# A hybrid decoder layer on one core: 4 KB of descriptor scratch instead of 16, and one to four more buffers for five kinds of tiles

## The chip, the core and the metric

The kernel runs on one core of a Trainium2 chip. The core has a matrix engine (TensorE, PE in the profile, with PEld for the loading of its weights), VectorE (DVE), ScalarE (ACT), GpSimd (POOL) and SyncE (SP), which each work through their own instructions in order and wait for each other by semaphores. DMAs are issued from the queues of SP, ACT and POOL and run on 16 DMA engines. The metric is the device time of one execution in microseconds; less is better.

## The reference, cut to what matters

One inference step of a decoder layer for a prompt (1024 tokens) and for 8 samples with 4 new tokens each. Each sample has a past of 8192 keys in pages of 128 that lie scattered in a pool. The attention has three branches: compressed blocks, the 16 best blocks of 64 keys, and a sliding window.

```python
def compress(k, pe, w1, w2):
    ...
    per = jnp.einsum('bcjgd,rjdh->rbcgh', kc, w1r)
    ...
    return jax.nn.silu(h) @ w2
...
    _, idx = lax.top_k(score, n_top)
    ...
    k_sel = ks_bg[b_i, g_i, idx].reshape(B, N_KV, Q, n_sel, HEAD_DIM)
    v_sel = vs_bg[b_i, g_i, idx].reshape(B, N_KV, Q, n_sel, HEAD_DIM)
...
    q, kv, g_nsa, g_a, glu, g_b, g_mrg = split_cols(xn @ w_in, SPLITS)
```

So all the past keys and values of every sample are read page by page and compressed (the first cost), and the chosen blocks are gathered again from other pools (the second). Beside that stand one wide projection of 1056 tokens by `w_in`, a depthwise convolution, and the output products. Products in 32 bits are made of three: the operand is split into a rounded part ("h") and the rest ("l"), and hh, hl and lh are added.

## The kernel before

The program is written out as straight code, with a scheduler that sets the order of each engine's instructions from a timeline of its own and from priorities (`high_priority`). It knows how many buffers a tile has: a tile with the tag X and `bufs=N` may exist N times, and the instruction that fills the next one waits until the last reader of the oldest is done.

Stage one (up to about 530 us in the trace) weaves two streams (line 890). `units` compresses the samples' pages: the keys of samples 0 to 3, their values, the keys of samples 4 to 7, the choice of blocks, their values. `fill1` makes the first projections of `w_in`. In `compress` (line 509) one sample's keys or values are 16 gathers. A gather (line 573) is an indirect DMA of POOL that fills a tile `G` of 128 rows by 512 numbers, of which there are GB. VectorE transposes it (line 531) into a quarter of `T` (two buffers); ScalarE rounds the four quarters into `Th` (line 535); VectorE subtracts them for `Tl` (line 539); TensorE then makes 24 products `x<-Th` or `x<-Tl` (line 521). 64 such groups of four gathers make up the eight samples. VectorE's order of these is pulled forward (HD at line 530).

A projection (`project`, line 250) loads 128 columns of `w_in` into `wt` on SP's queue (line 247), splits them into `wh` (ScalarE) and `wl` (VectorE), and makes 72 products `mm<-xh,wh`, `mm<-xl,wh`, `mm<-xh,wl` (lines 192 to 194).

Stage two (about 530 to 870 us) weaves the samples' selected and window attention, more projections, and the convolution's taps on VectorE (line 1264). Selected keys are gathered by POOL into `KG` (KB buffers, line 1043), ScalarE takes out one group's half into `kg` (K2 buffers, line 1046), and TensorE transposes it (line 1049). Values come into `VG`. The window's keys are loaded by SP into `wk` (WK buffers, line 962) and transposed on TensorE (line 968). From there on the prompt's attention, the merge and the output follow; none of the tiles whose buffers change is used after the last projections, in the first part of the prompt's attention.

## Time and profile before

| what | value |
| --- | --- |
| median of 3 runs | 1442.09 us (1439.83 to 1443.89) |
| the profiled execution | 1445.79 us, of which 1444.0 lie between its first and its last instruction |
| PE busy | 1349.5 us (93%), PEld 1206.3 (84%) |
| DVE busy | 1081.8 us (75%) |
| ACT busy | 721.4 us (50%) |
| POOL busy | 656.4 us (45%) |
| bytes moved by DMA | 256.86 MB, of which 125.85 by POOL's queue |

A row of a group gives line, engine, operation, what it writes and reads, its shape and count, then its busy time and the mean of one in ns, then the idle time of the engine ahead of it and what ended that. "x<-Tl,w1hk" writes x and reads Tl and w1hk. A row of waits gives who waited for whom, the total in us, how often, and the longest. A busy PE is not PE at its peak, since products overlap and their ends are modelled.

### The profile page before, as it was taken

To read this page: it belongs to the slowest core of one execution; us is meant where nothing else is said; L and a number is where in the kernel's file an instruction comes from. 1 tells how busy PE (TensorE), PEld (TensorE's weight loads), DVE (VectorE), ACT (ScalarE), POOL (GpSimd) and SP (SyncE) were. 2 spreads that over 40 slices of the span, in tenths; PEclk is the share of its full clock that TensorE was granted. 3 is DMA by queue.
4 is the path that set the end of the run, shared out by engine and by line. 5 is a ranking of instruction groups with operands and counts; after the bars stand their busy time and mean duration, and the time that the engine had idled before them with its cause. 6 is when DMAs were issued, how large, how long until landed. Compare 5 with 4: busy or idle time off the path is not lost.

```text
span 1444.0 us, 25602 instructions
## 1 busy us (share of the span) xinstructions
PE 1349.5 (93%) x9689; PEld 1206.3 (84%) x9689; DVE 1081.8 (75%) x1915; ACT 721.4 (50%) x1323; POOL 656.4 (45%) x537
## 2 busy tenths in 40 slices
PE   5999989979998999999999999999969999899997
PEld 4987889978898999878787889888958899789876
DVE  7787887787887765979864943978777987888233
ACT  5444455454442542445555424777656776653311
POOL 1477775777777434455544401444474221321200
PEclk9999999999999999999999999999989999999999
DMA  7565567556656536697878656533573632416421
GB/s 238 164 203 170 176 177 217 187 173 201 200 172 209 164 91 224 209 321 258 298 281 302 215 160 170 171 113 106 151 193 96 197 119 91 140 29 216 171 96 47
DMA packets 184357, 256.86 MB, mean 178 GB/s; under 512 B 27347, under 2 KB 137507, under 8 KB 183970
## 3 DMA queue, kind: packets, MB, share of 16 engines
q1 hardware_dynamic: 137114, 121.42, 28.1%
q0 software_dynamic: 36608, 125.85, 26.4%
q10 hardware_dynamic: 10512, 7.96, 1.8%
q8 instruction: 76, 1.25, 0.4%
q14 instruction: 47, 0.39, 0.1%
HBM read 215.56 MB, written 44.20 MB: 180 GB/s over the span
## 4 chain that ended last, share of the span: by engine, by line
PE 54%; DMA 15%; DVE 12%; issue 8%; POOL 6%; ACT 2%; SPq 2%; ACTq 0%; DVEq 0%; POOLq 0%
POOL G L573 6%; PE mm L192 5%; PE mm L194 5%; PE mm L193 5%; DMA G<-in_cache_k_cmp,idxc 5%; DMA G<-in_cache_v_cmp,idxc 4%; PE v L192 3%; PE v L194 3%; PE v L193 3%; PE tr L192 3%; PE tr L194 3%; PE tr L193 3%; DVE T L531 3%; PE tr L1512 2%; PE x L1032 2%
## 5 line engine op out<-in xcount | busy, mean ns | idle before, releaser
L192 PE MATMUL mm<-xh,wh 128*128 128x352 f32 x840 | 278.7, 332 | 3.6 <-DVE stg L284 2.0
L193 PE MATMUL mm<-xl,wh 128*128 128x352 f32 x840 | 275.3, 328 | 0.7 <-DVE xl L407 0.7
L194 PE MATMUL mm<-xh,wl 128*128 128x352 f32 x840 | 275.8, 328 | 0.0
L531 DVE STREAM_TRANSPOSE T<-G 128x512 f32<-128x512 f32 x260 | 175.2, 697 | 81.0 <-DMA G<-in_cache_k_cmp,idxc 38.6
L573 POOL DMA_INDIRECT G<-in_cache_k_cmp,idxc x128 | 164.7, 1287 | 99.5 <-DMA w2bk<-in_w_k 34.5
L573 POOL DMA_INDIRECT G<-in_cache_v_cmp,idxc x128 | 174.3, 1362 | 78.2 <-DVE T L531 45.4
L535 ACT ACTIVATE Th<-T 128x2048 fp32r<-128x2048 f32 x66 | 124.7, 1890 | 168.0 <-DVE T L531 123.1
L192 PEld LDWEIGHTS mm<-xh,wh 128*128 128x128 f32 x840 | 159.9, 190 | 13.1 <-issue 7.4
L194 PEld LDWEIGHTS mm<-xh,wl 128*128 128x128 f32 x840 | 159.9, 190 | 7.0 <-issue 6.7
L193 PEld LDWEIGHTS mm<-xl,wh 128*128 128x128 f32 x840 | 160.2, 191 | 6.5 <-issue 4.8
L1227 DVE SCALAR_TENSOR_TENSOR acc<-ub,dwT,acc 128x1024 f32<-128x1024 f32 x120 | 154.3, 1286 | 1.1
L539 DVE TENSOR_TENSOR Tl<-T,Th 128x2048 fp32r<-128x2048 f32 x66 | 146.9, 2225 | 3.0 <-ACT Th L535 2.9
L1335 DVE TENSOR_TENSOR ptl<-tr,pth 128x512 fp32r<-128x512 f32 (+1 forms) x152 | 100.3, 670 | 21.5 <-ACT pth L1334 20.5
L1426 ACT ACTIVATE P<-S,sc 128x640 f32<-128x640 f32 (+7 forms) x128 | 89.2, 701 | 36.8 <-PE tr L1512 19.1
L1334 ACT ACTIVATE pth<-tr 128x512 fp32r<-128x512 f32 (+1 forms) x152 | 87.6, 585 | 37.0 <-PE tr L1512 29.4
L1019 POOL DMA_INDIRECT KG<-in_cache_k_slc,idxs x56 | 66.0, 1179 | 81.9 <-ACT kg L1046 60.8
L1487 POOL TENSOR_SCALAR P<-P,sc 128x640 f32<-128x640 f32 (+4 forms) x32 | 53.0, 1656 | 109.7 <-DVE sc L1480 79.6
L521 PE MATMUL x<-Tl,w1hk 128*128 128x256 f32 (+1 forms) x264 | 78.2, 296 | 15.1 <-DVE Tl L539 11.1
L521 PE MATMUL x<-Tl,w1hv 128*128 128x256 f32 (+1 forms) x264 | 79.0, 299 | 10.7 <-DVE Tl L539 10.7
L1019 POOL DMA_INDIRECT VG<-in_cache_v_slc,idxs x56 | 64.3, 1148 | 51.3 <-PE y L1104 33.8
L1503 PE MATMUL acc<-ptl,vs 128*128 128x256 f32 x264 | 73.7, 301 | 10.9 <-DVE ptl L1335 10.5
L1512 PE MATMUL tr<-ident,P 128*128 128x128 f32 x528 | 81.5, 280 | 1.7 <-ACT var L1613 0.6
(469 smaller groups left out, 3593.2 us busy)
## 6 DMA issues: line engine op xcount, KB each, us to landing
wt<-in_w_in SPq DMA_DIRECT2D x42, 512.0 KB
m_d<-stg SPq DMA_DIRECT2D x16, 528.0 KB
x<-in_x_prompt SPq DMA_DIRECT2D x16, 512.0 KB
mb<-m_d SPq DMA_DIRECT2D x24, 176.0 KB
t_d<-mb SPq DMA_DIRECT2D x24, 176.0 KB
mb<-t_d SPq DMA_DIRECT2D x24, 176.0 KB
ma<-m_d SPq DMA_DIRECT2D x24, 176.0 KB
ldq<-qT_d SPq DMA_DIRECT2D x32, 128.0 KB
```

The costliest lines, as they stand in the source:

```text
L192: pe.matmul(ps, wh, xh, start=i == 0, stop=False)
L193: pe.matmul(ps, wh, xl, start=False, stop=False)
L194: LAST_MM[0] = pe.matmul(ps, wl, xh, start=False, stop=i == n - 1)
L521: pe.matmul(o, w[:, s], t[:, :, :, s // 2, s % 2], start=s == 0 and i == 0, stop=s == 7 and i == 2)
L531: dve.transpose(T[:, gi], G)
L535: act.activation(Th[:, :m], T[:, :m], AF.Copy)
L539: eng.tensor_tensor(Tl[:, r], T[:, r], Th.bitcast(F32)[:, r], op=ALU.subtract)
L573: pool.indirect_dma_start(out=G, out_offset=None, in_=tab, in_offset=bass.IndirectOffsetOnAxis(ap=idxc[:, b * 16 + gi:b * 16 + gi + 1], ax ...
L1019: pool.indirect_dma_start(out=dst, out_offset=None, in_=pools[n], in_offset=bass.IndirectOffsetOnAxis(ap=col, axis=0))
L1227: eng.scalar_tensor_tensor(a, x, dwT[:, ct, j:j + 1], a, op0=ALU.mult, op1=ALU.add)
L1335: dve.tensor_tensor(lo[:, :w], t[:, :w], hi.bitcast(F32)[:, :w], op=ALU.subtract)
L1512: pe.transpose(t[:, (2 * x + e) * 128:(2 * x + e + 1) * 128], Ps[e * 2 + i][:, c0:c0 + 128], ident)
```

## The change

```diff
-GB = 4
+GB = 8
...
-WK = 1
+WK = 2
...
-KB = 3
-K2 = 2
+KB = 4
+K2 = 3
...
-        wt = wpl.tile([128, 8, 128], F32, name="wt", tag="wt")
+        wt = wpl.tile([128, 8, 128], F32, name="wt", tag="wt", bufs=3)
...
-    nc = _bacc.Bacc("TRN2", target_bir_lowering=False, num_devices=1)
+    nc = _bacc.Bacc("TRN2", target_bir_lowering=False, num_devices=1, dynamic_dma_scratch_size=4096)
```

Since the scheduler counts buffers, it also orders the instructions anew. On POOL the last 64 gathers of stage one, the values of samples 4 to 7, are cut by two index tables for the choice of blocks (IOTA) and two fills of the convolution's input (MEMSET):

```order
 L573 DMA G<-in_cache_v_cmp,idxc 128x512 x64
 L573 DMA G<-in_cache_k_cmp,idxc 128x512 x64
-L573 DMA G<-in_cache_v_cmp,idxc 128x512 x3
+L573 DMA G<-in_cache_v_cmp,idxc 128x512 x8
 L173 IOTA TC 64x64
 L173 IOTA TA 128x128
-L573 DMA G<-in_cache_v_cmp,idxc 128x512 x19
+L573 DMA G<-in_cache_v_cmp,idxc 128x512 x20
 L1188 MEMSET ub 128x30 x2
-L573 DMA G<-in_cache_v_cmp,idxc 128x512 x42
+L573 DMA G<-in_cache_v_cmp,idxc 128x512 x36
```

The gathers follow each other as before; eight instead of three stand ahead of the tables, and 28 instead of 22 ahead of the fills.

On VectorE, in the compression of the first samples' keys (T is the transposition of one G, Tl the subtraction for a group of four, H the sums at a sample's end, wl a projection's weights), before:

```order
L531 STREAM_TRANSPOSE T<-G 128x512
L562 TENSOR_TENSOR H<-x,H 64x255
L562 TENSOR_TENSOR H<-x,H 64x256
L531 STREAM_TRANSPOSE T<-G 128x512 x3
L539 TENSOR_TENSOR Tl<-T,Th 128x2048
L531 STREAM_TRANSPOSE T<-G 128x512
L256 TENSOR_TENSOR wl<-wt,wh 128x1024
L566 SCALAR_TENSOR_TENSOR H<-sg,H 128x511
L531 STREAM_TRANSPOSE T<-G 128x512
L565 MEMSET H 128x1
L531 STREAM_TRANSPOSE T<-G 128x512 x2
L539 TENSOR_TENSOR Tl<-T,Th 128x2048
```

and of the change:

```order
L562 TENSOR_TENSOR H<-x,H 64x255
L562 TENSOR_TENSOR H<-x,H 64x256
L531 STREAM_TRANSPOSE T<-G 128x512 x4
L539 TENSOR_TENSOR Tl<-T,Th 128x2048
L566 SCALAR_TENSOR_TENSOR H<-sg,H 128x511
L531 STREAM_TRANSPOSE T<-G 128x512 x4
L565 MEMSET H 128x1
L539 TENSOR_TENSOR Tl<-T,Th 128x2048
L256 TENSOR_TENSOR wl<-wt,wh 128x1024
```

Four transpositions now mostly stand in one run ahead of a Tl, where they were spread between other work. In the whole program there are 43 runs of exactly four, where there were 15, and 14 single ones, where there were 60.

## The prediction

> **What bounds the kernel now.** I read the busy time by stage first, because an average over the run mixes stages with different limits. The columns are stretch, its length, busy us (and count) of PE, PEld, DVE, ACT and POOL, granted clock, DMA share and GB/s.

> ```profile
> span 1444.0 us, 25602 instructions
> 50.00:530.00 480.00, 446.56 (x3145) 417.66 (x3144) 388.53 (x546) 223.47 (x283) 338.42 (x257) 0.97 0.61 186
> 530.00:870.00 340.00, 334.29 (x2995) 279.80 (x2994) 243.12 (x501) 153.56 (x302) 138.39 (x125) 1.00 0.72 244
> 870.00:1300.00 430.00, 400.44 (x2716) 367.18 (x2715) 348.57 (x611) 283.34 (x615) 159.71 (x137) 0.97 0.45 130
> 1300.00:1444.00 144.00, 134.94 (x646) 111.21 (x644) 65.07 (x152) 33.46 (x73) 14.60 (x6) 0.99 0.39 132
> ```

> The first stretch holds the compression of the pages, the second the gathers of the selected keys, the third and fourth the prompt's attention and the output. In the second PE is idle for 5.7 us of 340: TensorE bounds it. In the first PE is idle for 33.4 us of 480 at a clock of 0.97, so something else holds it at times. The chain of waits in that stretch says what:

> ```profile
> by line: issue 19.5%; POOL G L573 16.9%; DMA G<-in_cache_k_cmp,idxc 15.4%; DMA G<-in_cache_v_cmp,idxc 11.0%; DVE T L531 8.3%; PE x L521 5.8%; DVE Tl L539 4.8%; PE mm L192 2.7%; PE mm L193 2.7%; PE mm L194 2.6%; DMA ct_d<-tk 2.5%; SPq L583 1
> ```

> Gathers and their landings are 43% of that chain and PE's lines only some 14%. The waits of the stretch close the loop: VectorE's transposition waits for a landed G, and POOL waits for that transposition before it may refill the buffer.

> ```profile
> L531 DVE STREAM_TRANSPOSE T<-G 128x512 f32<-128x512 f32 x260 | 175.2, 697 | 81.0 <-DMA G<-in_cache_k_cmp,idxc 38.6 <-DMA G<-in_cache_v_cmp,idxc 31.6 <-DMA G<-ct_d 5.1
> POOL G L573 <- DVE T L531: 73.5, 71, 16.6
> POOL G L573 <- issue: 47.2, 141, 2.2
> ```

> The price on TensorE is the idle time ahead of its compression products (line 521):

> ```profile
> L521 PE MATMUL x<-Tl,w1hk 128*128 128x256 f32 (+1 forms) x264 | 78.2, 296 | 15.1 <-DVE Tl L539 11.1 <-issue 3.9
> L521 PE MATMUL x<-Tl,w1hv 128*128 128x256 f32 (+1 forms) x258 | 77.3, 300 | 10.7 <-DVE Tl L539 10.7
> L521 PE MATMUL x<-Th,w1hk 128*128 128x256 f32 (+1 forms) x264 | 77.1, 292 | 0.6 <-ACT Th L535 0.4 <-issue 0.2
> ```

> That is 15.1 + 10.7 + 0.6 = 26.4 us of the 33.4. So the stage is bound by TensorE, with a page loop just behind it that holds it up for 26 us.

> **The change, part by part.**

> *Eight buffers for G instead of four.* This is the part that counts. First, is POOL fast enough to use them? Its gathers in this stage:

> ```profile
> L573 POOL DMA_INDIRECT G<-in_cache_v_cmp,idxc x128 | 174.3, 1362 | 78.2 <-DVE T L531 45.4 <-issue 24.1 <-DMA G<-in_cache_v_cmp,idxc 3.2
> L573 POOL DMA_INDIRECT G<-in_cache_k_cmp,idxc x124 | 160.4, 1294 | 57.5 <-DVE T L531 28.1 <-issue 23.1 <-DMA G<-in_cache_k_cmp,idxc 2.6
> L573 POOL DMA_INDIRECT G<-in_cache_v_cmp,idxc x128: 943/949/3261, 154.9 to 516.8; - x128
> ```

> The 252 gathers from 50 us on run for 174.3 + 160.4 = 334.7 us. The timeline has at least 0.30 us between two, so POOL needs 334.7 + 252 x 0.30 = 410 us. It took 467 (50 to 516.8, the last row's end of starts). PE, without its 26.4 us, needs 453.6 for the stage. POOL without waits is thus 10% faster than TensorE wants. Where it is fed without a break, it shows that pace, 12 gathers in 17.4 us, 1.45 us each:

> ```profile
> 340.94 0.95 POOL L573 DMA_INDIRECT G<-in_cache_k_cmp,idxc  x1 [0.31 <-issue]
> ...
> 358.32 2.03 POOL L573 DMA_INDIRECT G<-in_cache_k_cmp,idxc  x1 [0.30 <-issue]
> ```

> Second, is the buffer loop what slows it? The chain has, from the start of a gather to its landing,

> ```profile
> 340.94 3.57 DMA G<-in_cache_k_cmp,idxc
> 103.87 5.59 DMA G<-in_cache_k_cmp,idxc
> ```

> To this come 0.30 us ahead of it and 0.70 us of transposition (mean 697 ns), with no queueing on VectorE: 4.6 to 6.6 us a turn. Four buffers give one gather per 1.15 to 1.65 us, which straddles POOL's own 1.45; any queueing makes the buffers the limit, and the mean was 467 / 252 = 1.85. Eight buffers give 0.57 to 0.82, well under POOL's pace. So the loop goes, and what is late next is POOL itself, 10% ahead of PE. As that margin is thin and comes in bursts, I take two thirds of the 26.4 us, **17.6 us**. Ends: 0 and 26.4.

> *The clock.* 0.97 over 480 us is 14.4 us of TensorE lost. Two windows show that it is tied to waiting only loosely: one with PE busy 44.2 of 50 us keeps the full clock, one with 20.6 of 25 loses it.

> ```profile
> 100.00:150.00 50.00, 44.21 (x369) 35.87 (x362) 39.32 (x51) 21.95 (x26) 36.55 (x28) 1.00 0.56 179
> 450.00:475.00 25.00, 20.58 (x117) 20.00 (x116) 20.83 (x47) 8.76 (x15) 15.13 (x12) 0.86 0.69 212
> ```

> I take half, **7.2 us**; ends 0 and 14.4.

> *KG four for three, kg three for two, wk two for one.* POOL waits much for a free KG, 60.8 us, but the products that read kg and wk hardly wait at all:

> ```profile
> POOL KG L1019 <- ACT kg L1046: 60.8, 20, 7.4
> L1049 PE MATMUL tr<-ident,kg 128*128 128x128 f32 x224 | 35.2, 279 | 0.9 <-issue 0.9
> L968 PE MATMUL tr<-ident,wk 128*128 128x128 f32 x32 | 5.1, 283 | 0.0
> ```

> The cover is TensorE's full load in 530 to 870; the stage cannot give more than its 5.7 us. I take **0**; ends: a gain of 5.7, and as large a loss by DMAs that now start earlier (share 0.72 already).

> *Three wt for two.* SP's queue waits long for a free wt, and the projections that need it do not: their only idle time is 2.6 us in the first stage, put down to other tiles.

> ```profile
> SPq L247 <- DVE wl L256: 225.9, 23, 35.0
> L192 PE MATMUL mm<-xh,wh 128*128 128x352 f32 x408 | 134.5, 330 | 2.6 <-DVE stg L284 2.0 <-ACT stg L670 0.6
> ```

> Value 0. The loads move past a few neighbours on SP's queue (the copy of state_conv, the small loads of pe and w2), whose users are not late by the same rows; should one be, the price is a landing of some 5 us.

> *The scratch, 4 KB for 16.* No row shows POOL waiting for it, with at most four G, or three KG and four VG, under way. By the rows its cost is between 0 and what the third rival below works out; I take 0, since POOL's median gather (949 ns) takes no longer than its shortest (943 ns), so at least half of them wait for nothing, and the long ones lie beside VectorE's subtractions (first rival). [...]

> *Order.* TensorE's moves little: ahead of the last of the 64 full compression groups stand 1304 projection products before and 1321 after, ahead of the 16th 412 and 389. From the prompt's attention on, the orders of all five engines agree but for a few rows at its start, so the stretches after 870 us cost what they did.

> The sum is 17.6 + 7.2 = 24.8 us. Against the profiled execution's own 1445.79 us (span 1444.0) that is 1421.0. The median of the runs shown, 1442.09, lies 3.7 lower, and the forecast with it: **1417 us**.

> **The rivals.**

> *POOL stays the limit* (no change). A gather that meets VectorE's subtraction Tl is held up: one that started at 110.46 took 2.73 us and ended 0.8 us after Tl did.

> ```profile
> 110.46 2.73 POOL L573 DMA_INDIRECT G<-in_cache_k_cmp,idxc  x1 [1.02 <-DVE T L531]
> 110.12 2.25 DVE L539 TENSOR_TENSOR Tl<-T,Th 128x2048 fp32r<-128x2048 f32 x1
> L539 DVE TENSOR_TENSOR Tl<-T,Th 128x2048 fp32r<-128x2048 f32 x66 | 146.9, 2225 | 3.0 <-ACT Th L535 2.9
> L256 DVE TENSOR_TENSOR wl<-wt,wh 128x1024 fp32r<-128x1024 f32 x18 | 21.5, 1193 | 1.1 <-ACT wh L255 1.1
> ```

> Now 334.7 - 252 x 0.949 = 95.6 us are lost so, out of 146.9 + 21.5 = 168.4 of such subtractions. If a POOL that is always busy loses all of it, it needs 252 x 1.25 + 168.4 = 483 us, no less than now: 1441. Against it stands the stretch at 1.45 us. [...]

> *VectorE's order holds TensorE up* (slower). Of the runs of four transpositions there are 15 before and 43 after, so a Tl more often stands behind a whole group's four G. If gathers keep their 1.85 us, 28 more Tl wait one transposition longer, 28 x 0.70 = 20 us: 1462. It decides where a G comes slower than TensorE's 453.6 / 256 = 1.77 us. Against it: POOL's 410 / 252 = 1.63.

> *The scratch is too small* (the change then does not do what its buffers say). If POOL waits for one landing (3.6 us at best) with each 8 gathers, that is 31 x 3.6 = 112 us, of which its slack (467 - 410 = 57) hides half: 1442 + 55 = 1497.

> **How the numbers follow.** The forecast has 0.76, POOL as the limit 0.13, the order 0.08, the scratch 0.03. A measurement of this kernel tells about 0.3% (4.3 us) from no change. Faster is the forecast's 0.76, the same POOL's 0.13, slower 0.08 + 0.03 = 0.11. The forecast's best case is 26.4 + 14.4 + 5.7 = 46.5 us, 1396; its worst runs into the no-change case, whose upper edge is 1446. That range leaves out the slower cases and a little below it, some 0.15.

> **What would show it.** Right: ahead of line 521 PE waits under 10 us, POOL's wait for T falls from 73.5 below 30, the last gather starts near 490 us instead of 516.8, the mean gather grows a little (more of them meet a Tl), the clock of the stage is 0.98 or more, and the later stretches keep 340, 430 and 144 us. Wrong: a mean gather near 1.6 us with POOL never waiting (the first rival); T's wait for G still near 70 us with Tl behind it (the second); long gathers with no Tl beside them (the third).

## The result, and the profile after

The changed kernel takes 1417.53 us in the median of 4 runs (1414.06 to 1422.37), the kernel before 1441.93 (1439.83 to 1443.89) beside it: a ratio of 0.984, 95% interval 0.981 to 0.987. It is faster by 24 us. Run again twice, once with another scratch size and the same order of instructions, it gave 0.980 and 0.983.

The profiled execution took 1420.95 us. Its page and the table by stage come first. The columns are those of the table before; the bounds between stages follow the work, so that a stage that became shorter has a shorter row.

```profile
span 1419.2 us, 25556 instructions
PE 1337.1 (94%) x9689; PEld 1202.6 (85%) x9689; DVE 1078.7 (76%) x1915; ACT 720.5 (51%) x1323; POOL 646.0 (46%) x537
```

```profile
50.00:513.00 463.00, 440.45 (x3164) 418.45 (x3163) 386.32 (x548) 223.92 (x282) 324.00 (x253) 0.98 0.61 191
513.00:847.00 334.00, 331.49 (x2996) 278.88 (x2996) 244.47 (x501) 152.92 (x303) 138.57 (x125) 1.00 0.73 248
847.00:1277.00 430.00, 400.04 (x2716) 366.45 (x2716) 347.54 (x610) 283.19 (x615) 159.46 (x137) 0.97 0.45 131
1277.00:1420.00 143.00, 133.02 (x634) 109.28 (x632) 64.43 (x149) 32.99 (x73) 14.29 (x6) 0.98 0.38 128
```

Held against the four rows before (480, 340, 430 and 144 us), 17 us went from the compression of the pages, 6 from the stretch with the selected keys (which a second execution does not show, see the first experiments), none from the prompt's attention and 1 from the end. In the first, PE's idle time fell from 480 - 446.56 = 33.4 us to 463 - 440.45 = 22.6, and its busy time by 446.56 - 440.45 = 6.1 for about as many products. In the second, idle time fell from 5.7 to 2.5 us and busy time by 2.8.

The chain of waits of the first stage says what changed there:

```profile
by line: PE x L521 20.2%; issue 14.0%; POOL G L573 11.7%; DMA G<-in_cache_k_cmp,idxc 7.8%; PE mm L192 7.7%; PE mm L193 7.7%; PE mm L194 7.7%; DMA G<-in_cache_v_cmp,idxc 7.5%; DVE T L531 5.4%; DVE Tl L539 3.0%; DVE H L562 1.2%; PE tr L676 1.
```

Gathers and their landings were 43.3% of it and are 27.0% now; PE's own lines, 5.8 + 2.7 + 2.7 + 2.6 = 13.8% of it before, are 20.2 + 3 x 7.7 = 43.3%. TensorE is now the largest part of the chain. The rows that made the page loop, in the stage (50 to 530 us):

```profile
L531 DVE STREAM_TRANSPOSE T<-G 128x512 f32<-128x512 f32 x260 | 167.9, 686 | 38.1 <-DMA G<-in_cache_v_cmp,idxc 17.9 <-DMA G<-in_cache_k_cmp,idxc 16.9 <-DMA G<-ct_d 1.4
POOL G L573 <- issue: 47.3, 156, 0.3
POOL G L573 <- DVE T L531: 46.9, 45, 20.5
POOL G L573 <- DMA G<-ct_d: 16.0, 2, 9.5
L521 PE MATMUL x<-Tl,w1hk 128*128 128x256 f32 (+1 forms) x264 | 77.9, 295 | 5.1 <-DVE Tl L539 5.1
L521 PE MATMUL x<-Tl,w1hv 128*128 128x256 f32 (+1 forms) x264 | 77.6, 294 | 6.7 <-DVE Tl L539 6.7
L521 PE MATMUL x<-Th,w1hk 128*128 128x256 f32 (+1 forms) x264 | 77.1, 292 | 3.5 <-ACT Th L535 3.5
L521 PE MATMUL x<-Th,w1hv 128*128 128x256 f32 (+1 forms) x264 | 76.2, 289 | 2.5 <-issue 2.5
L573 POOL DMA_INDIRECT G<-in_cache_v_cmp,idxc x128 | 167.0, 1304 | 79.6 <-DVE T L531 29.1 <-issue 24.1 <-DMA G<-ct_d 16.0
L573 POOL DMA_INDIRECT G<-in_cache_k_cmp,idxc x120 | 155.2, 1293 | 47.7 <-issue 23.2 <-DVE T L531 17.8 <-DMA G<-in_cache_k_cmp,idxc 3.0
L573 POOL DMA_INDIRECT G<-in_cache_v_cmp,idxc x128: 943/949/4392, 143.2 to 497.2; - x128
L573 POOL DMA_INDIRECT G<-in_cache_k_cmp,idxc x120: 945/949/4776, 51.7 to 367.2; - x120
```

VectorE waits 34.8 us for a landed G where it waited 70.2, PE waits 5.1 + 6.7 + 3.5 + 2.5 = 17.8 us ahead of line 521 where it waited 26.4, and the last gather starts at 497.2 us, 19.6 earlier.

### The profile page after: what moved, and what is told of

Same layout as the page of the kernel before. It is cut to its first block, busy times and chain, and to the rows that moved or that the text cites. A ratio compares the mean times of both kernels' runs of the same rounds, so it can differ in the third digit from the quotient of the medians.

```text
span 1419.2 us, 25556 instructions
## 1 busy us (share of the span) xinstructions
PE 1337.1 (94%) x9689; PEld 1202.6 (85%) x9689; DVE 1078.7 (76%) x1915; ACT 720.5 (51%) x1323; POOL 646.0 (46%) x537
## 3 DMA queue, kind: packets, MB, share of 16 engines
q8 instruction: 76, 1.25, 0.3%
## 4 chain that ended last, share of the span: by engine, by line
PE 66%; DVE 11%; DMA 9%; issue 6%; POOL 4%; ACT 3%; SPq 1%; DVEq 0%; POOLq 0%; ACTq 0%
PE mm L193 7%; PE mm L192 7%; PE mm L194 7%; PE x L521 7%; POOL G L573 4%; PE v L192 3%; PE v L194 3%; PE v L193 3%; PE tr L192 3%; PE tr L194 3%; DMA G<-in_cache_k_cmp,idxc 3%; PE tr L193 3%; PE tr L1512 3%; DMA G<-in_cache_v_cmp,idxc 2%; PE x L1032 2%
## 5 line engine op out<-in xcount | busy, mean ns | idle before, releaser
L192 PE MATMUL mm<-xh,wh 128*128 128x352 f32 x840 | 276.4, 329 | 2.8 <-ACT xh L401 2.0
L193 PE MATMUL mm<-xl,wh 128*128 128x352 f32 x840 | 275.1, 327 | 0.9 <-DVE xl L407 0.9
L194 PE MATMUL mm<-xh,wl 128*128 128x352 f32 x840 | 274.7, 327 | 0.0
L573 POOL DMA_INDIRECT G<-in_cache_v_cmp,idxc x128 | 167.0, 1304 | 79.6 <-DVE T L531 29.1
L573 POOL DMA_INDIRECT G<-in_cache_k_cmp,idxc x128 | 163.8, 1280 | 86.4 <-DMA w2bk<-in_w_k 30.0
L531 DVE STREAM_TRANSPOSE T<-G 128x512 f32<-128x512 f32 x260 | 167.9, 686 | 38.1 <-DMA G<-in_cache_v_cmp,idxc 17.9
L535 ACT ACTIVATE Th<-T 128x2048 fp32r<-128x2048 f32 x66 | 124.7, 1889 | 94.6 <-DVE T L531 41.0
L193 PEld LDWEIGHTS mm<-xl,wh 128*128 128x128 f32 x840 | 159.0, 189 | 10.1 <-issue 8.3
L192 PEld LDWEIGHTS mm<-xh,wh 128*128 128x128 f32 x840 | 158.5, 189 | 9.3 <-issue 6.2
L194 PEld LDWEIGHTS mm<-xh,wl 128*128 128x128 f32 x840 | 158.7, 189 | 5.4 <-issue 4.9
L539 DVE TENSOR_TENSOR Tl<-T,Th 128x2048 fp32r<-128x2048 f32 x66 | 147.4, 2237 | 15.9 <-issue 9.5
L1019 POOL DMA_INDIRECT KG<-in_cache_k_slc,idxs x56 | 63.5, 1133 | 71.6 <-ACT kg L1046 53.8
L1019 POOL DMA_INDIRECT VG<-in_cache_v_slc,idxs x56 | 67.4, 1203 | 56.5 <-PE y L1104 37.3
L521 PE MATMUL x<-Tl,w1hv 128*128 128x256 f32 (+1 forms) x264 | 77.6, 294 | 6.7 <-DVE Tl L539 6.7
L521 PE MATMUL x<-Tl,w1hk 128*128 128x256 f32 (+1 forms) x264 | 77.9, 295 | 5.1 <-DVE Tl L539 5.1
```

The lines of the kernel that those rows point to most:

```text
L192: pe.matmul(ps, wh, xh, start=i == 0, stop=False)
L193: pe.matmul(ps, wh, xl, start=False, stop=False)
L194: LAST_MM[0] = pe.matmul(ps, wl, xh, start=False, stop=i == n - 1)
L521: pe.matmul(o, w[:, s], t[:, :, :, s // 2, s % 2], start=s == 0 and i == 0, stop=s == 7 and i == 2)
L531: dve.transpose(T[:, gi], G)
L535: act.activation(Th[:, :m], T[:, :m], AF.Copy)
```

## The experiments

### Eight G buffers alone, all the rest alone, the scratch alone

The first takes from the change GB and the scratch; the second everything but GB; the third the scratch alone.

```diff
 e1_g8:      GB = 8, dynamic_dma_scratch_size=4096
 e2_rest:    GB = 4, WK = 2, KB = 4, K2 = 3, wt bufs=3, dynamic_dma_scratch_size=4096
 e3_scratch: dynamic_dma_scratch_size=4096
```

> The scratch at 4 KB and eight G buffers; all other buffers as before. Theory (the page loop in the first 530 us was the price, the other buffers give nothing): 1416 to 1424 us, the whole gain or all but some 2 us of it; PE's wait ahead of line 521 falls from 26.4 to under 15 us, and the last gather starts near 497 us as in the changed kernel. Rival (the 5 us by which the selected-key stage and the start of the prompt's attention became shorter come from the KG, kg, wk and wt buffers): 1421 to 1427 us, with the stretch from the first transposition of kg to the first product of the prompt's compressed scores at 324 us as before, not at 319.

> The scratch at 4 KB, one more wt, KG, kg and wk; G keeps its four buffers. Theory (these are worth nothing): 1438 to 1446 us, the last gather near 517 us, POOL's wait for T near 73 us. Rival (they give the 5 us of the later stage, or the order that they bring does): 1434 to 1438 us, with that stage at 319 us for 324.

> The scratch alone at 4 KB; no buffer is added, and the order of every engine's instructions is that of before. Theory (the size of the scratch has no price here): 1438 to 1446 us, POOL's mean gather of G 1.29 to 1.36 us as before. Rival (a smaller scratch costs or gains by itself): outside of that, with gathers that are long with no subtraction beside them if it costs.

| kernel | median us | ratio to the kernel before, 95% interval |
| --- | --- | --- |
| eight G buffers | 1422.56 | 0.985 (0.982 to 0.988) |
| the other buffers | 1446.21 | 1.001 (0.998 to 1.003) |
| the scratch | 1441.63 | 0.999 (0.997 to 1.001) |

Eight G buffers are the whole gain, within what can be told; the other buffers and the smaller scratch are worth nothing. The time with eight buffers lies in both ranges that were expected. PE waits 6.8 + 6.8 + 4.4 = 18.0 us ahead of line 521 there, more than the 15 expected, and the last gather starts at 491.3 us. With the other buffers alone POOL's wait for T (70.1 us) and the last gather (518.1 us) stay near those of before, and with the scratch alone the mean gather does (1.30 us). In the same 480 us, with eight G buffers TensorE is busy for 460.36 us with 3314 products, and it was for 446.56 with 3145:

```profile
50.00:530.00 480.00, 460.36 (x3314) 436.69 (x3313) 391.59 (x556) 231.65 (x299) 329.58 (x254) 0.98 0.60 185
```

Whether the 6 us of the second stretch belong to the change can be read from when the first transposition of kg (line 1049) and the first score of the prompt (line 1375) start. First the kernel before, then the changed one, then the changed one in its second run (`e11_after` below), then eight G buffers alone, then the other buffers alone:

```profile
L1049 PE MATMUL tr<-ident,kg x224: 270/272/331, 566.2 to 806.5; 128*128 128x128 f32 x112
L1375 PE MATMUL S<-kcb,qp x64: 270/275/418, 890.8 to 1043.4; 128*128 128x128 f32 x64
```

```profile
L1049 PE MATMUL tr<-ident,kg x224: 270/273/330, 548.0 to 782.3; 128*128 128x128 f32 x112
L1375 PE MATMUL S<-kcb,qp x64: 270/275/356, 867.4 to 1019.2; 128*128 128x128 f32 x64
```

```profile
L1049 PE MATMUL tr<-ident,kg x224: 270/273/330, 548.0 to 790.1; 128*128 128x128 f32 x112
L1375 PE MATMUL S<-kcb,qp x64: 270/275/422, 875.6 to 1028.3; 128*128 128x128 f32 x64
```

```profile
L1049 PE MATMUL tr<-ident,kg x224: 270/273/333, 542.9 to 786.7; 128*128 128x128 f32 x112
L1375 PE MATMUL S<-kcb,qp x64: 270/275/356, 869.4 to 1021.2; 128*128 128x128 f32 x64
```

```profile
L1049 PE MATMUL tr<-ident,kg x224: 270/273/476, 566.6 to 805.3; 128*128 128x128 f32 x112
L1375 PE MATMUL S<-kcb,qp x64: 270/275/356, 890.6 to 1042.4; 128*128 128x128 f32 x64
```

Between the two marks lie 324.6, 319.4, 327.6, 326.5 and 324.0 us. The changed kernel itself takes 319.4 us in one execution and 327.6 in another, so the 6 us are no more than executions of one kernel differ, and no gain of that stretch is shown. What the two executions share is the first mark, 548.0 us. It stands 18.2 us ahead of that of the kernel before, and 12.5 ahead of the 560.5 us of the kernel with the scratch alone, whose buffers are those of before. So what the traces show for certain is a gain of 12 to 18 us ahead of the first mark, in the first stage; where the rest of the 24 lies is open.

### The changed kernel with less scratch

With the changed kernel's order of instructions and 512 or 1024 bytes of scratch in place of 4096:

```diff
-dynamic_dma_scratch_size=4096
+dynamic_dma_scratch_size=512     (e4_s512)
+dynamic_dma_scratch_size=1024    (e5_s1024)
```

> The changed kernel with 512 bytes of scratch instead of 4096, in the same order of instructions. [...] Rival (the scratch does not limit the gathers under way at all): 1414 to 1422 us as the changed kernel, mean gather 1.29 us.

> The changed kernel with 1024 bytes of scratch instead of 4096. With 512 bytes the whole gain was lost (ratio 1.0004) and the idle time ahead of the gathers that the profile puts down to issue rose from 47.3 to 88.4 us between 50 and 530. Theory one: the scratch holds the descriptors of the gathers that are under way, and twice as many fit as with 512; about 60 us of 128 gathers lie between two landings of 1.25 us each, so that with twice the room the pace of 1.25 us is held and this kernel is the changed one again: 1414 to 1422 us, ratio 0.981 to 0.987, issue near 47 us. Rival: descriptors under way need more room than 1024 bytes in the densest stretches, so that part of the loss stays: 1425 to 1438 us, issue 55 to 80 us, single waits above 2 us.

With 512 bytes the kernel takes 1443.95 us, ratio 1.000 (0.998 to 1.003); with 1024 it takes 1417.93, ratio 0.980 (0.976 to 0.984). The whole gain is lost and comes back. The 1024 bytes came out as expected, with 48.9 us of gaps put down to "issue" and none over 0.3. With 512 bytes the rival's 1414 to 1422 us did not come. The price lies below the 1497 us of the prediction's third rival, and it doesn't show as the long gathers by which that rival was to be told. The waits of POOL with 512 bytes, and some of its gathers in order of time (start, us, and in brackets the idle time ahead):

```profile
POOL G L573 <- issue: 88.4, 177, 4.7
POOL G L573 <- DVE T L531: 33.2, 36, 14.9
```

```profile
160.51 0.94 POOL L573 DMA_INDIRECT G<-in_cache_v_cmp,idxc  x1 [0.46 <-issue]
162.64 1.16 POOL L573 DMA_INDIRECT G<-in_cache_v_cmp,idxc  x1 [1.19 <-issue]
...
169.22 0.94 POOL L573 DMA_INDIRECT G<-in_cache_v_cmp,idxc  x1 [1.45 <-issue]
```

Most gathers keep their 0.94 or 0.95 us, their mean is (160.4 + 149.4) / 248 = 1.25 us where the changed kernel has 1.30, and the gap between two, which is 0.30 us where nothing holds POOL, grows to as much as 4.7 without a name. 177 gaps at 0.30 would be 53 us; the 35 us above that came with the 512 bytes, against 47.3 - 156 x 0.30 = 0.5 us in the changed kernel and 48.9 - 161 x 0.30 = 0.6 with 1024. VectorE waits for a landed G much as before the change, 35.0 + 27.5 = 62.5 us:

```profile
L531 DVE STREAM_TRANSPOSE T<-G 128x512 f32<-128x512 f32 x260 | 171.2, 691 | 65.7 <-DMA G<-in_cache_k_cmp,idxc 35.0 <-DMA G<-in_cache_v_cmp,idxc 27.5 <-DMA G<-ct_d 1.4
```

Since order and buffers are those of the changed kernel, this answers a question that the buffers alone leave open: GB also changes the scheduler's order, and **the new order alone does not bring the gain; it needs a POOL that can run ahead**. A kernel with eight buffers whose POOL is held for 35 us between gathers is as slow as one with four (1.000 and 0.999). Whether more gathers under way bring the gain in the old order too was not tried. By their times 512 bytes (1.000) behave like four buffers and not like five (0.988), 1024 (0.980) like six (0.979) or more (next). How many gathers are under way with 512 bytes no run shows; should they be fewer than with the four buffers of before, a small gain of the order could be hidden in that run.

### Five, six and ten buffers

```diff
-GB = 4
+GB = 5    (e10_g5)
+GB = 6    (e6_g6)
+GB = 10   (e7_g10 and e12_g10)
```

All with 4096 bytes of scratch and none of the other buffers.

> The kernel before with six G buffers and 4096 bytes of scratch, nothing else. Theory one (a buffer is held by a gather from its issue to its transposition, and what counts is how far POOL may run ahead of VectorE): the gain comes in steps, most of it with the first two buffers more: 1424 to 1432 us, POOL's wait for T at L531 between 50 and 60 us against 73.5 with four and 38.9 with eight, last gather starting between 495 and 508 us. Rival (only a run-ahead of two whole groups of four counts, since VectorE takes the transpositions in groups of four): six buffers bring little, 1436 to 1443 us, last gather after 510 us.

> The kernel with eight G buffers alone, now with ten. Theory one: with eight, POOL is held by its own pace (1.25 us a gather and 2 to 3 us where VectorE's subtraction runs beside it) and by the two waits for ct_d, no longer by the number of buffers: 1416 to 1424 us, same as with eight, and the PE waits ahead of line 521 stay between 12 and 20 us. Rival: buffers still bind, since POOL still waits 38.9 us for T with eight: 1409 to 1415 us, POOL's wait for T below 28 us, last gather before 486 us.

> The kernel before with five G buffers and 4096 bytes of scratch, nothing else. Six, eight and ten gave ratios of 0.979, 0.985 and 0.977, four 0.999. Theory one (run-ahead beyond one group of four is what counts, and the first buffers bring most): half the gain or more, 1424 to 1434 us, with POOL's wait for T at L531 between 58 and 72 us. Rival (a second group's gathers must be well under way while VectorE takes the first, so a single buffer more is not enough): 1437 to 1444 us.

> The changed kernel once more, beside ten G buffers on the same chip, since the spread from chip to chip and from call to call is as large as what is between six, eight and ten buffers. Theory one (two buffers more than eight change nothing that can be told): ratio 0.979 to 0.985, within 0.003 of that of ten. Rival: ten are better by 0.003 or more.

> Ten G buffers and 4096 bytes of scratch, none of the other buffers, once more. Theory one: the same as the changed kernel, 0.979 to 0.985. Rival (as the earlier run of it, 0.977, and its clock of 0.984 in place of 0.979 would have it): 0.974 to 0.978, with PE idle and busy time both below those of the changed kernel.

| G buffers | median us | ratio to the kernel before, 95% interval |
| --- | --- | --- |
| 4 (the scratch alone) | 1441.63 | 0.999 (0.997 to 1.001) |
| 5 | 1426.52 | 0.988 (0.984 to 0.993) |
| 6 | 1415.53 | 0.979 (0.975 to 0.983) |
| 8 | 1422.56 | 0.985 (0.982 to 0.988) |
| 8, the changed kernel, again | 1420.65 | 0.983 (0.979 to 0.987) |
| 10 | 1413.16 | 0.977 (0.973 to 0.980) |
| 10, beside the changed kernel | 1426.65 | 0.988 (0.983 to 0.993) |

By the medians five buffers bring more than half, six all of it. Five came out as expected, with a wait of POOL for T of 58.4 us. Six gave more than expected, though POOL's wait for T (58.3 us) was as expected. Ten had the rival's time once (1413.16 us), but not its signs (POOL's wait for T is 39.4 us and the last gather starts at 488.6); the other time, beside the changed kernel, they were hardly better than five, above what either theory had, while the changed kernel's 0.983 was as expected. So between six and ten nothing can be told apart, and no version was found that is surely faster than the changed kernel. The saturation is in line with the prediction's turn of a buffer: 4.6 to 6.6 us over six buffers are 0.77 to 1.10 us a gather, less than the 1.25 that POOL needs for one that nothing holds up (0.95 and 0.30); over five they are 0.92 to 1.32, on both sides of it. That is no proof: held against the 1.45 us that the prediction took as POOL's pace five would do, and the chain of before also has single landings of 6.03 and 7.54 us, which make longer turns.

### Buffers of their own for the prompt's tiles

After one of 20.5 us for T, the longest waits left to POOL in the changed kernel are two for `ct_d`: SP fills four tiles of the same rotation for the prompt's compression, and a gather further on waits until such a tile has landed and been read.

```profile
224.83 2.25 POOL L573 DMA_INDIRECT G<-in_cache_v_cmp,idxc  x1 [6.50 <-DMA G<-ct_d]
244.94 0.95 POOL L573 DMA_INDIRECT G<-in_cache_v_cmp,idxc  x1 [9.54 <-DMA G<-ct_d]
```

```diff
 GB = 8, dynamic_dma_scratch_size=4096, and
-G = cpl.tile([128, 512], F32, name="G", tag="G", bufs=GB)
+G = cpl.tile([128, 512], F32, name="G", tag="G" if n > 2 else "GP", bufs=GB if n > 2 else 2)
```

> Eight G buffers alone, with two buffers of their own for the four tiles of the prompt's compression, which SyncE loads from ct_d and which stood in the rotation of G. In the kernel with eight G buffers POOL waits 16.5 us in two pieces for ct_d there. Theory one: those waits go, gathers behind them start 10 to 16 us earlier, and PE loses 3 to 6 us less in the stage, since part of its idle time lies elsewhere: 1414 to 1419 us. Rival: PE has other work in that stretch (300 product groups stand in its order before the late gathers are needed), so the end of the stage stays: 1419 to 1424 us, last gather between 486 and 492 us, with POOL's wait moved to T at L531.

It takes 1415.39 us, ratio 0.978 (0.974 to 0.982), beside 0.980 (0.976 to 0.984) of the changed kernel with 1024 bytes on the same chip: not to be told apart. (Eight G buffers alone, 0.985, ran on another chip.) The waits for ct_d are gone, and POOL waits for T instead, 55.3 us where eight buffers alone had 38.9; the last gather does not start earlier (493.6, and 491.3 with eight buffers alone).

```profile
POOL G L573 <- DVE T L531: 55.3, 49, 20.7
```

```profile
L573 POOL DMA_INDIRECT G<-in_cache_v_cmp,idxc x128: 942/946/5353, 145.2 to 493.6; - x128
```

PE's waits ahead of line 521 are 8.6 + 6.5 + 3.6 = 18.7 us, and 18.0 with eight buffers alone. The time is one that theory one allowed, but neither the earlier gathers nor the shorter waits of PE that it asked for came. What came is the rival's move of the wait to T; by these rows the wait for ct_d had been slack.

### Without the subtraction

```diff
-eng.tensor_tensor(Tl[:, r], T[:, r], Th.bitcast(F32)[:, r], op=ALU.subtract)
-Tl = cpl.tile([128, 4, 512], F32R, name="Tl", tag="Tl")
+Tl = Th
```

> The changed kernel without the subtraction Tl = T - Th of the compression (L539): Th stands in its place in the products, so that TensorE's products are the same in number and size, the output is that of a coarser split, and VectorE has 66 subtractions of 2.2 us less in the stage. Theory one (a gather is longer than 0.95 us only where one of VectorE's long subtractions runs beside it, and such a gather is what makes the page loop late in the changed kernel): the mean gather falls from 1.30 to at most 1.05 us, PE's idle time ahead of line 521 from about 15 us to under 6, the last gather starts before 480 us, and the run takes 1396 to 1410 us, since PE idles only 22.5 of 455 us in the stage. Rival (the long gathers come from the DMA side, from its queues being full): the mean gather stays above 1.2 us and the time within 6 us of the changed kernel's.

One half came out and the other did not. From 50 to 530 us the gathers take

```profile
L570 POOL DMA_INDIRECT G<-in_cache_v_cmp,idxc x128 | 124.5, 972 | 121.9 <-DVE T L531 88.2 <-issue 22.7 <-DVE H L559 7.6
L570 POOL DMA_INDIRECT G<-in_cache_k_cmp,idxc x120 | 115.3, 961 | 87.5 <-DVE T L531 57.8 <-issue 25.2 <-DMA G<-in_cache_k_cmp,idxc 1.8
L570 POOL DMA_INDIRECT G<-in_cache_v_cmp,idxc x128: 940/946/1770, 141.4 to 497.8; - x128
L570 POOL DMA_INDIRECT G<-in_cache_k_cmp,idxc x120: 940/946/1857, 51.7 to 384.9; - x120
```

a mean of 0.97 us where the changed kernel has 1.30, and none over 1.86: the long gathers are those beside VectorE's subtraction, some 80 us of POOL in this stage (322.2 - 239.8). The changed kernel's own trace says the same: of its 65 gathers over 1.1 us in these 480 us, 63 overlap a subtraction Tl or wl. The longest meets two Tl in a row:

```profile
367.21 4.78 POOL L573 DMA_INDIRECT G<-in_cache_k_cmp,idxc  x1 [0.30 <-issue]
366.70 4.46 DVE L539 TENSOR_TENSOR Tl<-T,Th 128x2048 fp32r<-128x2048 f32 x2
```

But the run is slower, 1485.31 us, ratio 1.029 (1.023 to 1.034). PE waits 19.6 + 1.8 + 15.4 + 0.2 = 37.0 us ahead of line 521, where under 6 were expected, and the last gather starts at 497.8 us and not before 480. The chain of waits in its first stage, its row of the table, and two of its waits:

```profile
by line: PE x L521 40.0%; issue 13.4%; PE mm L194 8.9%; PE mm L192 8.7%; PE mm L193 8.5%; another core or an unknown queue 4.9%; PE mm L635 2.5%; ACT Th L535 2.4%; DVE T L531 2.2%; PE tr L673 1.4%; PE y L714 1.0%; PE tr L739 0.8%; DVE wl L2
50.00:530.00 480.00, 415.99 (x2830) 382.90 (x2831) 237.69 (x475) 213.24 (x270) 240.37 (x252) 0.91 0.56 174
DVE T L531 <- ACT Th L535: 91.1, 19, 11.5
PE x L521 <- issue: 34.6, 52, 1.7
```

PE is idle for 64 us of the 480 at a clock of 0.91, and the products of line 521 are the largest part of the chain. The scheduler gave the engines another order here. VectorE's transposition now waits for ScalarE's Th, where in the changed kernel 36.2 of its 38.1 us are waits for a landed G, and most of PE's idle time ahead of line 521 has no name. What made the run slower was not taken apart. So the time of this run says nothing of the subtraction's price, and what it would bring to lift POOL's pace in the changed kernel stays open.

## Why the prediction was right, and where its steps were not

The granted clock over the whole run, before and after:

```profile
core 0: 1444.0 us, clock 0.980
```

```profile
core 0: 1419.2 us, clock 0.979
```

The predicted 1417 us stand beside 1417.53. The mechanism that carries the forecast holds, but that the sum comes out to within 1 us is luck: the first stage gave 17 us in the profiled execution where the forecast had all its 24.8, and some 7 came from stretches for which it had 0.

- **Eight G buffers.** The step that carries the forecast holds: G buffers alone are the gain (0.985), the loop through POOL's refill was what held the stage, and a POOL that can run ahead is needed for it (512 bytes of scratch, with 35 us of longer gaps between gathers, undo it: 1.000). The term was mis-sized: of PE's idle time in the stage 33.4 - 22.6 = 10.8 us went, not 17.6, and ahead of line 521 there stay 17.8 us where under 10 were to stay. The last gather starts at 497.2 us and was to start near 490. The turn of 4.6 to 6.6 us was taken from two landings of 3.57 and 5.59 us; the same chain has others of 6.03 and 7.54.
- **The clock.** 0.97 over 480 us was 14.4 us, 0.98 over 463 is 9.3, so about 5 of the 7.2 came in the stage (two digits say no more; PE's busy time there fell by 6.1). Over the run the clock is 0.980 before and 0.979 after, 28.9 and 29.8 us lost: what the stage gained was lost elsewhere, some 3.5 us of it in the first 50 us (1.00 before, 0.93 after). In its second run the changed kernel has 1.00 there too and 0.981 over the whole, so where the clock is lost differs between executions of one kernel. As a term of the whole run it was nought.
- **The later stretches.** The third row kept its 430 us and the fourth lost 1. The second was to keep 340 and lost 6, just over the end of 5.7 that stood beside the value of 0. In this execution that makes up for most of what the first stage brought too little, but the second run of the changed kernel takes 327.6 us between the two marks where this one takes 319.4 and the kernel before 324.6. So it is not shown to come from the change. The value of 0 for KG, kg, wk and wt as edits stands (1.001 alone).
- **The scratch.** 0 at 4096 bytes, by itself (0.999) and within the change (1024 bytes are as good). A scratch that is too small has a price, at 512 bytes (1.000 for 0.984), but what was to show it was wrong: not long gathers, but unnamed gaps of up to 4.7 us between gathers of 0.95. How the scratch holds POOL up no run shows.
- **POOL as the limit.** It did not stay the limit; its 1.45 us in a row and the mean of 1.63 with the gap were better guides than the rival's sum. The mean gather was to grow a little and fell, from 1.33 to (167.0 + 155.2) / 248 = 1.30 us.
- **VectorE's order.** The second rival needed T's wait for G to stay near 70 us; it is 34.8.
- **POOL's wait for T** was to fall below 30 us and fell to 46.9. This signal contradicted the prediction's own numbers: if POOL needs 410 us and PE 454, POOL must wait about 44 us for something. What tells that the loop is gone is VectorE's wait for G and the chain, not POOL's wait.

Not tried: an order like that of before with eight buffers. By the rows 11.8 of the remaining 17.8 us ahead of line 521 are waits for Tl; what makes Tl late was not taken apart by a run.

## What to carry to other kernels

Divide the turn of a buffer (issue, landing, the reader, and the gap) by the number of buffers and hold it against the pace of the engine that fills it: that tells about how many buffers help (here six by the medians), and more brought nothing that could be told. Judge by the engine that sets the end: when an engine is let run ahead, its own waits must stay as large as its slack, and a long one that only moved from one name to another, as that for ct_d did, brought nothing here. A forecast in several terms is to be held against the profile term by term, since some 8 us too much in one stage and 7 too little elsewhere looked like a hit. And a few us of one stage are to be read from more than one execution of the same kernel.

## What the runs showed of the hardware

- What a scratch of 512 bytes costs shows nowhere by name. Most gathers keep their 0.95 us, and the gap ahead of them, put down to "issue", grows from 0.30 us to as much as 4.7; the sum of such gaps less their count times 0.30 us is the measure (35 us with 512 bytes, 0.6 with 1024, 0.5 with 4096). A few us of it prove nothing: the kernel before, with four buffers and 16384 bytes, has 47.2 - 141 x 0.30 = 4.9.
- A gather is as short as 0.94 us and had a mean of 0.97 where VectorE ran no long subtractions of the compression. In the changed kernel, from 50 to 530 us, the 117 gathers that overlap a subtraction Tl or wl have a mean of 1.69 us and single ones took up to 4.8; the other 131 have a mean of 0.95. Which step of a gather it is that waits no run here shows.
- A clock of 0.91 over the compression came with a TensorE that was busy for 416 of 480 us, in the kernel without the subtraction; 0.97 came with 447 of 480.
